# A hybrid diffusion layer on one core: the MLP's scale as a factor per partition, and two transposes moved into the output projection

## Chip, core and metric

The kernel runs on one core of a Trainium2 chip. The metric is the device time of one execution in microseconds (us). The engines are named as in the profile: PE (matrix products and transposes, with PEld for its weight loads), DVE (vector), ACT (scalar), POOL, and SP, which only issues DMAs here; ACT issues a few as well.

## What is computed

One layer over 512 latent tokens of width 1024 with 256 context tokens. Two sub-layers follow each other: attention beside a state-space scan with a common output projection, then a gated MLP with a width-3 convolution along the tokens on the gate.

```python
mix_x = jnp.concatenate([attn_x, ssd_x], axis=-1) @ w_out[l]           # (512, 2048) @ (2048, 1024)
x = x + mod_x[2] * rms_norm(mix_x, mix_post_norm[l])
ffn_x = conv_glu(modulate(rms_norm(x, ffn_pre_norm[l]), mod_x[3], mod_x[4]),
                 w_up[l], ffn_conv_w[l], ffn_conv_b[l], w_down[l])
x = x + mod_x[5] * rms_norm(ffn_x, ffn_post_norm[l])

def rms_norm(x, w):     # y = x * rsqrt(mean(x*x) + EPS) * w
def modulate(h, shift, scale):
    return h * (1 + scale) + shift
```

`mod_x[i]` are six vectors of 1024 that one matrix-vector product makes from the conditioning vector: 2 is the mixer's gate, 3 the MLP's shift, 4 the MLP's scale, 5 the MLP's gate. All is float32.

## The kernel before

**Precision.** A float32 operand of a large product is split into two parts, hi and lo, in a format that PE takes at full rate (`split`, L497 on ACT makes hi, L498 on DVE makes lo), and a product is the sum of hi·hi, hi·lo and lo·hi.

**Order.** The program is built twice. The first build records every instruction; `plan` then gives each tile a place in SBUF and each engine an order, by list scheduling with costs and waits written into the kernel; the second build follows that order. So an edit anywhere can move instructions everywhere. Two means bind the plan: `pins` say that certain products of PE come after others, and the PSUM bank that a `pget` hands out is decided by the order of the code (a queue of free banks: `pfree` puts a bank at its end).

**The output projection** (`natural_gemm`, L1288) multiplies 16 blocks of the concatenated 2048 features with w_out. Its result lies token by token: four token blocks `i` of 128, each in one of the four PSUM buffers of 128x1024 (kind "a"). The last four of the 16 are kept back and run block by block, so that block 0 is finished before block 3; block 3's tail runs in two halves of 512 columns. One half of a tail is 12 products of 128x512.

**The modulation vectors** are made meanwhile on DVE, 24 dot products of 128x1024 (L586, with loads of 512 KB each), as columns: feature p of block j is at partition p, column j of `mod`. `modfinish` (L1273) adds the bias and the norm's weights. Where a vector is needed along the free axis, it becomes a row: a DMA on ACT's queue writes the column to DRAM in pieces of four bytes (L1282, `mod_rows<-mod`), another reads it back to all partitions (L1284, `block<-mod_rows`, 512 KB). Before, this is done for the mixer's gate (`rows[2]`) and the MLP's scale (`rows[4]`); the MLP's shift stays a column.

**After each token block** `after_mix` (L1365) takes the sum of squares of the projection on ACT (L1347), 1/sqrt by a power on POOL (L521) with a Newton step on DVE (L522 to L528), multiplies by the gate's row (L1360; for block 3's second half L1362 and L1363), adds the residual stream (L1375), which is also written to DRAM (`held_rows`), takes its sum of squares, and multiplies by that factor and by the scale's row (L1379) to `hn`.

**Into the MLP.** `transposes` (L1384) turns `hn` of one token block to features on partitions: eight transposes on PE (L1387) to a PSUM buffer, then for each of the eight feature blocks hi with the shift as bias on ACT (L1390) and lo on DVE (L1391), into `h2`. All transposes come in the code after the output projection. The MLP's first product (`up`, L758) runs for three column blocks of w_up over tokens 0 to 255 first and then over 256 to 511, so it begins when blocks 0 and 1 are in `h2`.

## Time and profile before

| | |
|---|---|
| median of 3 runs | 986.82 us (985.85 to 990.34) |
| profiled execution, first to last instruction | 986.9 us; its own time is not given apart, and the span is within 0.1 us of the median |
| mean granted clock of PE | 0.992 |
| PE, PEld busy | 98%, 84% |
| DVE, ACT, POOL busy | 69%, 51%, 27% |
| output projection's last product, MLP's first | 607.8 us, 611.5 us |

Busy shares are means over stages of different kinds. In a row of a group stand line, engine, operation, tiles, shapes and count, then the busy time, the mean of one in ns, and the idle time just before with its cause. In a timeline row stand start and length, and in brackets how long the engine was idle before and what ended that. A "DMA to landing" is from the issue to the last byte. Matmuls are pipelined, and one's own length (390 ns) is more than the distance to the next.

### The profile page before, as it was taken

How to read it: one execution, taken by the hardware profiler on the slowest of the kernel's cores; microseconds unless marked ns; L12 is line 12 of the kernel's file. 1: busy time of each engine (PE TensorE's matmuls, PEld its weight loads, DVE VectorE, ACT ScalarE, POOL GpSimd, SP SyncE). 2: the span in 40 equal slices, each digit the busy share in tenths (PEclk: the TensorE clock that was granted, in tenths of full speed). 3: DMA queues.
4: the chain of work that ended last, by engine and by line, in shares of the span. 5: the costliest groups of instructions: out<-in, count | busy, mean ns of one | idle time of the engine just before them, and what ended most of it. 6: DMA issues, size and time to landing. Idle time of an engine off the chain costs nothing. (4 is left out here: it accounts for less than half of the span.)

```text
span 986.9 us, 14324 instructions
## 1 busy us (share of the span) xinstructions
PE 964.1 (98%) x5213; PEld 824.1 (84%) x5213; DVE 685.7 (69%) x1181; ACT 500.8 (51%) x996; POOL 265.0 (27%) x238
## 2 busy tenths in 40 slices
PE   8999999999999999999999998999999999999997
PEld 8888888888878878889888887988888888888885
DVE  5999877896889999878789948925244342583504
ACT  4555347548569786878786114823232242652001
POOL 0002103756599986566440001000000000000000
PEclk8999999999999999999999999999999999999999
DMA  9923211012331341334577576332222312444422
GB/s 345 376 96 114 75 43 59 23 43 62 84 98 55 105 113 36 100 96 108 149 274 272 175 155 247 129 107 86 107 86 93 120 54 75 128 144 140 144 86 106
DMA packets 47542, 121.07 MB, mean 123 GB/s; under 512 B 9057, under 2 KB 12017, under 8 KB 47473
## 3 DMA queue, kind: packets, MB, share of 16 engines
q1 hardware_dynamic: 43744, 118.49, 37.4%
q10 hardware_dynamic: 3728, 1.68, 0.6%
q8 instruction: 41, 0.67, 0.3%
q14 instruction: 29, 0.23, 0.1%
HBM read 98.11 MB, written 6.30 MB: 106 GB/s over the span
## 5 line engine op out<-in xcount | busy, mean ns | idle before, releaser
L758 PE MATMUL banks<-block,block 128*128 128x512 f32 (+1 forms) x2132 | 449.7, 362 | 4.3 <-ACT block L1390 1.9
L758 PEld LDWEIGHTS banks<-block,block 128*128 128x128 f32 x2132 | 361.8, 190 | 65.6 <-ACT block L1390 2.1
L498 DVE TENSOR_TENSOR block<-block,block 128x512 fp32r<-128x512 f32 (+5 forms) x252 | 217.8, 890 | 105.3 <-ACT block L497 44.6
L497 ACT ACTIVATE block<-block 128x512 fp32r<-128x512 f32 (+4 forms) x252 | 180.7, 746 | 204.8 <-PE banks L1482 43.0
L521 POOL TENSOR_TENSOR smalls<-smalls,powers 128x1 f32<-128x1 f32 (+3 forms) x16 | 12.7, 792 | 507.0 <-DVE smalls L1466 359.3
L1482 PE MATMUL banks<-block,block 128*128 128x512 f32 x512 | 117.8, 389 | 0.0
L1482 PEld LDWEIGHTS banks<-block,block 128*128 128x128 f32 x512 | 96.1, 188 | 19.9
L1188 POOL TENSOR_TENSOR block<-block,smalls 128x768 f32<-128x768 f32 x64 | 95.4, 1498 | 51.9 <-DVE smalls L1187 32.7
L1181 PE MATMUL banks<-block,block 128*128 128x256 f32 (+1 forms) x384 | 95.3, 355 | 5.1 <-issue 1.9
L498 DVE TENSOR_TENSOR block<-banks,block 128x512 fp32r<-128x512 f32 (+1 forms) x156 | 83.2, 556 | 13.9 <-ACT block L497 12.5
L1295 PE MATMUL banks<-block,block 128*128 128x512 f32 x384 | 89.2, 390 | 0.0
L497 ACT ACTIVATE block<-banks 128x256 fp32r<-128x256 f32 (+1 forms) x156 | 74.0, 500 | 23.3 <-PE banks L1199 10.8
L1295 PEld LDWEIGHTS banks<-block,block 128*128 128x128 f32 x384 | 71.6, 188 | 14.7 <-DVE block L1236 0.2
L1181 PEld LDWEIGHTS banks<-block,block 128*128 128x128 f32 x384 | 59.7, 189 | 13.0 <-ACT block L1185 4.4
L1211 PE MATMUL banks<-block,block 128*128 128x256 f32 x384 | 68.7, 294 | 0.1
L1185 ACT ACTIVATE block<-banks,smalls 128x768 f32<-128x768 f32 x64 | 58.0, 907 | 14.4 <-DVE smalls L1183 10.1
L1183 DVE TENSOR_REDUCE smalls<-banks 128x1 f32<-128x768 f32 x64 | 60.8, 950 | 5.9 <-PE banks L1181 5.6
L586 DVE SCALAR_TENSOR_TENSOR block<-block,block 128x1024 f32<-128x1024 f32 x50 | 60.3, 1219 | 6.2 <-DMA block<-in_wmod_dram 6.1
L1199 PE MATMUL banks<-cst,block 128*128 128x128 f32 x384 | 63.2, 273 | 0.1
L1211 PEld LDWEIGHTS banks<-block,block 128*128 128x128 f32 x384 | 56.4, 189 | 4.6 <-ACT block L497 1.1
L793 DVE SCALAR_TENSOR_TENSOR block<-banks,cwh,block 128x510 f32<-128x510 f32 (+3 forms) x88 | 51.7, 621 | 11.3 <-ACT block L789 10.5
L1199 PEld LDWEIGHTS banks<-cst,block 128*128 128x128 f32 x384 | 46.5, 140 | 8.1 <-issue 2.2
(220 smaller groups left out, 1040.8 us busy)
## 6 DMA issues: line engine op xcount, KB each, us to landing
block<-in_wmod_dram SPq DMA_DIRECT2D x48, 512.0 KB, 6.2
block<-in_wup_dram SPq DMA_DIRECT2D x44, 512.0 KB, 4.5
block<-in_wdn_dram SPq DMA_DIRECT2D x44, 256.0 KB, 3.3
block<-block SPq DMA_DIRECT2D x32, 256.0 KB, 3.0
block<-in_wout_dram SPq DMA_DIRECT2D x16, 512.0 KB, 5.2
block<-block SPq DMA_DIRECT2D x56, 128.0 KB, 2.5
block<-in_wxbc_dram SPq DMA_DIRECT2D x12, 512.0 KB, 3.3
block<-in_wz_dram SPq DMA_DIRECT2D x16, 256.0 KB, 6.0
```

Of the source, the lines that this page charges most:

```text
L497: act(hi, src, AF.Copy)
L498: (lo_eng or V).tensor_tensor(out=lo, in0=src, in1=hi, op=ALU.subtract)
L586: V.scalar_tensor_tensor(out=junk, in0=wt, scalar=0.5, in1=vec, op0=ALU.mult, op1=ALU.mult, accum_out=acc)
L758: mm(po, lhsT=wf(k, pt[0]), rhs=xf(k, pt[1]), start=(k == 0 and pt == parts[0]), stop=(k == nk - 1 and pt == parts[-1]))
L1181: mm(sc[:, o : o + n], lhsT=q_[:, x_, qi * P : (qi + 1) * P], rhs=kk[:, y_, :], start=part == 0, stop=part == 2)
L1183: V.reduce_max(nm, sc[:, :T], axis=AX.X, negate=True)
L1185: act(pe, sc[:, :T], AF.Exp, bias=nm, scale=1.0, accum_out=sm_)
L1188: G.tensor_tensor(out=pe, in0=pe, in1=sm_.to_broadcast([P, T]), op=ALU.mult)
L1199: nc.tensor.transpose((tx if c < NX else tc_)[:, o : o + P], pe[:, s_ : s_ + P], ident)
L1211: mm(po[:, half * 256 : half * 256 + 256], lhsT=vst(c), rhs=rhs, start=(part == 0 and c == 0), stop=(part == 1 and c == NKT - 1))
L1295: mm(po[i][:, nh * 512 : nh * 512 + 512], lhsT=l[lp][:, i * P : (i + 1) * P], rhs=w[wp][:, nh * 512 : nh * 512 + 512], start=(k == 0 and l ...
L1482: mm(po[i], lhsT=l[lp][:, i * P : (i + 1) * P], rhs=w[wp], start=(k == 0 and lp == 0 and wp == 0), stop=(k == NF - 1 and lp == 1))
```

## The change

There are four parts.

1. The MLP's scale (with ffn_pre_norm and 1 added) stays a column. `hn` is now only the normed stream, a multiplication by one factor per token (a TENSOR_SCALAR, L1383), and scale and shift are applied at the transposes' outputs, where features lie on partitions: one ACTIVATE with both columns to a new tile `ht` (L1394). The two DMAs for that row are gone.
2. hi and lo of `h2` are made from `ht` on DVE, for two feature blocks at a time, by a cast (L1398) and a subtraction (L1399). For that, `h2`'s tiles hold hi of two feature blocks or lo of two, in place of hi and lo of one.
3. `natural_gemm` calls `ahead` in front of each half of block 3's tail: the transposes of block 0 in front of the first half and those of block 1 in front of the second. Pins keep them there: the transposes come ahead of their half, and the second half behind the first. With that, block 0's and 1's transposes take the projection's buffers of blocks 0 and 1, and the MLP's first two column blocks get those of blocks 2 and 0, where they got those of blocks 2 and 3.
4. `rsqrt` puts half of its argument in a column of its own, so that DVE need not wait until POOL has read the argument.

```diff
     def rsqrt(x, n):
-        yt, tt = small(f"ry{n}", n), small(f"rt{n}", n)
+        yt, tt, xh = small(f"ry{n}", n), small(f"rt{n}", n), small(f"rh{n}", n)
         G.tensor_tensor(out=yt, in0=x, in1=powers[:, :n], op=ALU.pow)
-        V.tensor_scalar(out=x, in0=x, scalar1=-0.5, scalar2=None, op0=ALU.mult)
+        V.tensor_scalar(out=xh, in0=x, scalar1=-0.5, scalar2=None, op0=ALU.mult)
...
         for i in range(NX):
-            at.append(len(nc.cur_bb.bb.instructions))
-            cut = here()
-            for halves in (range(2),) if i < NX - 1 else ((0,), (1,)):
-                if halves == (1,):
-                    pins.append(((cut, here()), (here(), here() + 3 * len(tail))))
+            group, cut = [], here()
+            for n, halves in enumerate((range(2),) if i < NX - 1 else ((0,), (1,))):
+                between = here()
+                if i == NX - 1:
+                    ahead(n)
+                began = here()
                 for k, w, l in tail:
                     one(k, i, w, l, halves)
-            at[-1] = at[-1], len(nc.cur_bb.bb.instructions)
+                group.append((began, here()))
+                pins.extend(((o, o + 1), group[-1]) for o in range(between, began))
+            pins.extend(zip(group, group[1:]))
+            at.append((cut, here()))
             done(i, po[i])
...
         for h in cuts:
-            V.scalar_tensor_tensor(out=hn[:, h], in0=x1[i][:, h], scalar=c1, in1=rows[4][:, h], op0=ALU.mult, op1=ALU.mult)
+            V.tensor_scalar(out=hn[:, h], in0=x1[i][:, h], scalar1=c1, scalar2=None, op0=ALU.mult)
...
+        ht = t4(P, KD, P)
         for k in range(KD):
-            hi, lo, b = h2[k][:, 0, i * P : (i + 1) * P], h2[k][:, 1, i * P : (i + 1) * P], mod[:, 24 + k : 25 + k]
-            act(hi, tp[:, k * P : (k + 1) * P], AF.Identity, bias=b)
-            V.scalar_tensor_tensor(out=lo, in0=tp[:, k * P : (k + 1) * P], scalar=b, in1=hi, op0=ALU.add, op1=ALU.subtract)
+            act(ht[:, k], tp[:, k * P : (k + 1) * P], AF.Identity, scale=mod[:, 32 + k : 33 + k], bias=mod[:, 24 + k : 25 + k])
         pfree(tp)
+        for k in range(0, KD, 2):
+            hi, lo = (h2[k + p_][:, :, i * P : (i + 1) * P] for p_ in range(2))
+            V.tensor_copy(hi, ht[:, k : k + 2])
+            V.tensor_tensor(out=lo, in0=ht[:, k : k + 2], in1=hi, op=ALU.subtract)
...
-                rows[src] = modfinish(n, src, add, nrm, src != 3)
-
-    natural_gemm(16, lambda k: weight(a["wout"][korder[k]]), out_operand, after_mix, beside_out, keep=4)
+                rows[src] = modfinish(n, src, add, nrm, src == 2)
+
+    natural_gemm(16, lambda k: weight(a["wout"][korder[k]]), out_operand, after_mix, beside_out, keep=4,
+                 ahead=lambda n: transposes(*tails[n]))
...
-    h2v = lambda k, p_: h2[k][:, p_, :]
+    h2v = lambda k, p_: h2[k // 2 * 2 + p_][:, k % 2, :]
...
-    transposes(*tails[0])
-    transposes(*tails[1])
```

What the plan makes of it is shown at three places. PE before, at the end of the output projection (L1295), where block_916 is block 0's `hn`, block_920 block 1's, and L758 the MLP:

```order
L1295 MATMUL banks<-block_900_5539,block_879_5483 128x512
L1295 MATMUL banks<-block_901_5540,block_879_5483 128x512
L1295 MATMUL banks<-block_900_5539,block_888_5521 128x512
L1387 MATMUL banks<-cst,block_916_5584 128x128 x4
L1387 MATMUL banks<-cst,block_920_5621 128x128 x4
L1387 MATMUL banks<-cst,block_916_5584 128x128 x4
L1387 MATMUL banks<-cst,block_920_5621 128x128 x4
L758 MATMUL banks<-block_876_5478,block_935_5771 128x256
L758 MATMUL banks<-block_876_5478,block_941_5829 128x256
```

PE after, at the first transposes (L1391, block_915 is block 0's `hn`):

```order
L1295 MATMUL banks<-block_497_3054,block_696_4427 128x512
L1295 MATMUL banks<-block_875_5474,block_680_4345 128x512
L1295 MATMUL banks<-block_899_5535,block_902_5539 128x512 x2
L1295 MATMUL banks<-block_497_3054,block_697_4428 128x512
L1295 MATMUL banks<-block_876_5475,block_680_4345 128x512
L1391 MATMUL banks<-cst,block_915_5581 128x128 x4
L1295 MATMUL banks<-block_660_4179,block_697_4428 128x512
L1295 MATMUL banks<-block_875_5474,block_878_5478 128x512
L1391 MATMUL banks<-cst,block_915_5581 128x128 x4
L1295 MATMUL banks<-block_848_5367,block_654_4136 128x512
```

Block 0's transposes stood behind every product of the projection; now 38 products stand behind them. Block 1's stand 14 products ahead of the end. Behind the end (the first of the rows below is the last product), the MLP begins with four products, and then block 2's transposes follow (block_925 is its `hn`):

```order
L1295 MATMUL banks<-block_899_5535,block_902_5539 128x512
L758 MATMUL banks<-block_497_3054,block_942_5826 128x256
L758 MATMUL banks<-block_497_3054,block_936_5769 128x256
L758 MATMUL banks<-block_497_3054,block_939_5774 128x256
L758 MATMUL banks<-block_497_3054,block_945_5831 128x256
L1391 MATMUL banks<-cst,block_925_5666 128x128 x4
```

Before, block 2's first transposes stood behind 27 products of the MLP. Block 3's stand behind 59 products and block 2's eight transposes now.

ACT before, from the gate's scatter on (block_808 receives the gate's row, block_727 the scale's; L497 makes hi of w_out in block_900 and of w_up in block_935 and block_941; L1347 is a sum of squares):

```order
L1282 DMA mod_rows<-mod 128x8x1
L497 ACTIVATE block_900_5539<-block_779_5074 128x1024
L1347 ACTIVATE block_789_5114,smalls<-banks 128x1024
L1282 DMA mod_rows<-mod 128x8x1
L1284 DMA block_808_5191<-mod_rows 128x1024
L497 ACTIVATE block_935_5771<-block_809_5193 128x1024
L1284 DMA block_727_4691<-mod_rows 128x1024
L497 ACTIVATE block_941_5829<-block_744_4752 128x1024
```

ACT after (block_792 receives the gate's row; block_936 and block_942 are hi of w_up; L1351 is the sum of squares):

```order
L497 ACTIVATE block_897_5531<-block_715_4583 128x512
L1282 DMA mod_rows<-mod 128x8x1
L1351 ACTIVATE block_715_4583,smalls<-banks 128x1024
L497 ACTIVATE block_936_5769<-block_114_661 128x1024
L497 ACTIVATE block_942_5826<-block_799_5154 128x1024
L1284 DMA block_792_5143<-mod_rows 128x1024
L1351 ACTIVATE block_797_5150,smalls<-banks 128x1024
L497 ACTIVATE block_939_5774<-block_789_5113 128x1024
```

Of four DMAs two are left, and two conversions of w_up stand between the gate's scatter and its broadcast now.

DVE before, from the gate's row to block 0's `hn` (block_916; L1360 multiplies by the row, L1375 adds the residual stream, L1379 makes `hn`; the single-column rows are the Newton steps):

```order
L1360 TENSOR_TENSOR block_798_5151<-banks,block_808_5191 128x1024
L1375 SCALAR_TENSOR_TENSOR block_798_5151<-block_798_5151,smalls,block_715_4582 128x1024
L498 TENSOR_TENSOR block_936_5772<-block_809_5193,block_935_5771 128x1024
L1349 TENSOR_SCALAR smalls<-smalls 128x1
L522 TENSOR_SCALAR smalls<-smalls 128x1
L524 SCALAR_TENSOR_TENSOR smalls<-smalls 128x1
L528 SCALAR_TENSOR_TENSOR smalls<-smalls 128x1
L1349 TENSOR_SCALAR smalls<-smalls 128x1
L1360 TENSOR_TENSOR block_918_5612<-banks,block_808_5191 128x1024
L522 TENSOR_SCALAR smalls<-smalls 128x1
L1379 SCALAR_TENSOR_TENSOR block_916_5584<-block_798_5151,smalls,block_727_4691 128x1024
```

DVE after, the last part of the same stretch (ahead of it stand L1364 and L1379 of block 0, the first by the row, the second the residual stream's addition; L1383 makes `hn`):

```order
L1364 TENSOR_TENSOR block_843_5333<-banks,block_792_5143 128x1024
L524 SCALAR_TENSOR_TENSOR smalls<-smalls 128x1
L1353 TENSOR_SCALAR smalls<-smalls 128x1
L528 SCALAR_TENSOR_TENSOR smalls<-smalls 128x1
L522 TENSOR_SCALAR smalls<-smalls 128x1
L1379 SCALAR_TENSOR_TENSOR block_843_5333<-block_843_5333,smalls,block_597_3790 128x1024
L524 SCALAR_TENSOR_TENSOR smalls<-smalls 128x1
L498 TENSOR_TENSOR block_943_5827<-block_799_5154,block_942_5826 128x1024
L528 SCALAR_TENSOR_TENSOR smalls<-smalls 128x1
L1353 TENSOR_SCALAR smalls<-smalls 128x1
L1383 TENSOR_SCALAR block_915_5581<-block_818_5230,smalls 128x1024
```

Block 1's addition of the residual stream (L1379 after, L1375 before) now stands ahead of block 0's `hn`; there are six operations of 1024 columns from the row to `hn` where there were five.

More of the change, by code (lines that the diff above doesn't have):

```diff
@@ L518, in rsqrt @@
     def rsqrt(x, n):
-        yt, tt = small(f"ry{n}", n), small(f"rt{n}", n)
+        yt, tt, xh = small(f"ry{n}", n), small(f"rt{n}", n), small(f"rh{n}", n)
         G.tensor_tensor(out=yt, in0=x, in1=powers[:, :n], op=ALU.pow)
-        V.tensor_scalar(out=x, in0=x, scalar1=-0.5, scalar2=None, op0=ALU.mult)
+        V.tensor_scalar(out=xh, in0=x, scalar1=-0.5, scalar2=None, op0=ALU.mult)
         if n == 1:
-            V.scalar_tensor_tensor(out=tt, in0=yt, scalar=yt, in1=x, op0=ALU.mult, op1=ALU.mult)
+            V.scalar_tensor_tensor(out=tt, in0=yt, scalar=yt, in1=xh, op0=ALU.mult, op1=ALU.mult)
         else:
             V.tensor_tensor(out=tt, in0=yt, in1=yt, op=ALU.mult)
-            V.tensor_tensor(out=tt, in0=tt, in1=x, op=ALU.mult)
+            V.tensor_tensor(out=tt, in0=tt, in1=xh, op=ALU.mult)
         V.scalar_tensor_tensor(out=yt, in0=tt, scalar=1.5, in1=yt, op0=ALU.add, op1=ALU.mult)
@@ L1285, in modfinish, with natural_gemm @@
         return row
-    def natural_gemm(nk, wf, lf, done, beside_=lambda k: None, keep=4):
+    def natural_gemm(nk, wf, lf, done, beside_=lambda k: None, keep=4, ahead=lambda n: None):
         po = [pget("a") for _ in range(NX)]
@@ L1403, in beside_out @@
             if k == 4 * n + 3:
-                rows[src] = modfinish(n, src, add, nrm, src != 3)
-    natural_gemm(16, lambda k: weight(a["wout"][korder[k]]), out_operand, after_mix, beside_out, keep=4)
+                rows[src] = modfinish(n, src, add, nrm, src == 2)
+    natural_gemm(16, lambda k: weight(a["wout"][korder[k]]), out_operand, after_mix, beside_out, keep=4,
+                 ahead=lambda n: transposes(*tails[n]))
     gT = []
     EARLY = 3
-    h2v = lambda k, p_: h2[k][:, p_, :]
+    h2v = lambda k, p_: h2[k // 2 * 2 + p_][:, k % 2, :]
     def up(j, pu, ws, lo, hi):
         for s_ in range(2):
-            gemm_T(blk(ws[s_]), KD, ((pu[:, s_ * 512 + lo : s_ * 512 + hi], lambda k, p_: h2[k][:, p_, lo:hi]),))
+            gemm_T(blk(ws[s_]), KD, ((pu[:, s_ * 512 + lo : s_ * 512 + hi], lambda k, p_: h2v(k, p_)[:, lo:hi]),))
     def gated(j, gate, other, used):
```

## The prediction

> **What bounds the kernel now.** I read the page first, then busy time by stretch, then the PE timeline where a stretch falls short, then the chain that ended last to see what that place waits for.
>
> ```profile
> span 986.9 us, 14324 instructions
> PE 964.1 (98%) x5213; PEld 824.1 (84%) x5213; DVE 685.7 (69%) x1181; ACT 500.8 (51%) x996; POOL 265.0 (27%) x238
> L1295 PE MATMUL banks<-block,block 128*128 128x512 f32 x384 | 89.2, 390 | 0.0
> ```
>
> PE is busy for 964.1 of 986.9 us, so the end is set by PE's work and by the places where PE stands still or runs slowly. In the output projection it loses nothing: 384 products in 89.2 us, 0.232 us each. The stretches around the step from there to the MLP (columns: length, PE, PEld, DVE, ACT, POOL, then the granted clock):
>
> ```profile
> 600.00:605.00 5.00, 5.00 (x23) 4.13 (x23) 3.99 (x9) 2.15 (x4) 0.55 (x1) 1.00 0.75 238
> 605.00:610.00 5.00, 4.67 (x29) 3.87 (x27) 3.61 (x8) 2.40 (x4) 0.55 (x1) 1.00 0.58 230
> 610.00:615.00 5.00, 1.75 (x5) 1.26 (x6) 3.83 (x10) 2.93 (x10) 2.17 (x3) 0.76 0.95 336
> 615.00:620.00 5.00, 5.00 (x29) 5.00 (x27) 4.26 (x15) 4.56 (x15) 0.72 (x2) 0.55 0.36 143
> 620.00:625.00 5.00, 5.00 (x44) 4.94 (x42) 5.00 (x15) 4.52 (x12) 0.00 (x0) 1.00 0.08 9
> 625.00:630.00 5.00, 5.00 (x44) 5.00 (x43) 5.00 (x15) 4.69 (x12) 0.00 (x0) 1.00 0.93 369
> ```
>
> ```profile
> 599.81 8.10 PE L1295 MATMUL banks<-block,block 128*128 128x512 f32 x35
> 607.75 1.91 PE L1387 MATMUL banks<-cst,block 128*128 128x128 f32 x16
> 611.53 0.39 PE L758 MATMUL banks<-block,block 128*128 128x256 f32 x1 [1.87 <-ACT block L1390]
> 613.23 0.79 PE L758 MATMUL banks<-block,block 128*128 128x256 f32 x2 [1.31 <-DVE block L1360]
> 614.43 5.35 PE L758 MATMUL banks<-block,block 128*128 128x256 f32 x24 [0.40 <-DVE block L1391]
> ```
>
> Here lies what can be won. At 607.75 the last product is out, 16 transposes of blocks 0 and 1 follow, and then PE has nothing it may do: it waits 1.87 us for the first eviction, 1.31 us for a bank that block 3's reader still holds, 0.40 us for a low part. After these gaps the clock is 0.55 until 620, and matmuls come at 29 per 5 us instead of 44. From 610 to 625 there are 5 + 29 + 44 = 78; at 44 per 5 us they need 8.9 us, so 6.1 us are lost, with the 0.33 idle before 610 **6.5 us**. That is the ceiling of the main term. The chain says what comes before it:
>
> ```profile
> 563.79 10.08 DMA mod_rows<-mod
> 573.89 17.18 DMA block<-mod_rows
> ...
> 623.90 236.28 PE banks L758 x1154
> ```
>
> The mixing gate's row goes out as a column at 563.79 and comes back as a broadcast at 591.07. All of after_mix hangs on that arrival; from 623.9 on PE is the chain.
>
> **The second row.** The MLP's scale no longer becomes a row: one scatter, one broadcast and the two waits on ACT for them go.
>
> ```profile
> 571.54 1.30 SPq L489 DMA_DIRECT2D block<-in_wup_dram  x1
> ```
> ```profile
> 571.79 0.37 ACTq L1282 DMA_DIRECT2D mod_rows<-mod  x1
> ...
> 583.03 1.06 ACT L497 ACTIVATE block<-block 128x1024 fp32r<-128x1024 f32 x1 [10.69 <-DMA block<-in_wup_dram]
> 590.63 0.34 ACTq L1284 DMA_DIRECT2D block<-mod_rows  x1
> 591.09 1.06 ACT L497 ACTIVATE block<-block 128x1024 fp32r<-128x1024 f32 x1 [7.00 <-DMA mod_rows<-mod]
> ```
> ```profile
> DMA to landing us min/median/max: 6.0/11.0/18.8
> ```
>
> The last row is that of the tile mod_rows. The first broadcast's 17.2 us ended within half a microsecond of the second scatter, which stood ahead of it in ACT's queue (571.79 to 590.6). The broadcast that had nothing ahead took 6.0. So the remaining one should take about 6.0 to 6.5 instead of 17.2. But it starts later, for two reasons. In DVE's new order one L586, one L498 of 1024 and one of 512 more stand ahead of the gate's last factor (1.22 + 1.22 + 0.7 = 3.1 us): scatter at 567.0. And in ACT's new order two conversions of w_up stand between scatter and broadcast, where before there was none; ACT takes these in turn, so the broadcast waits for a load. Loads hardly move after a scatter; these two stretches of 4 us, from 572 and from 580, show it:
>
> ```profile
> DMA packets 19, 0.08 MB, mean 19 GB/s; under 512 B 0, under 2 KB 0, under 8 KB 19
> ...
> DMA packets 797, 1.46 MB, mean 365 GB/s; under 512 B 441, under 2 KB 441, under 8 KB 797
> ```
>
> Of before, the load issued at 571.54, the fourth in that jam, landed as its reader started, at 583.0: 19.2 after the scatter. After, the load that ACT needs is the third (or the second) of the jam; at 0.5 MB per 365 GB/s each place is 1.4 us. So it lands at 567.0 + 19.2 - 1.4 = 584.8 at the latest, and if loads move as soon as the scatter lands (10.08) at 567.0 + 10.1 + 3 x 1.4 = 581.3. Plus one conversion (1.06) and 6.0 to 6.5: the row arrives between **588.4 and 592.4**; I take 591.3, nearer the late end, since the jam is a row and its early end is not.
>
> **From the row to the first transposes.** DVE's rows for the steps between:
>
> ```profile
> L498 DVE TENSOR_TENSOR block<-block,block 128x1024 fp32r<-128x1024 f32 x77 | 93.5, 1225 | 43.7 <-PE banks L758 23.3 <-ACT block L497 18.0 <-issue 1.8
> L586 DVE SCALAR_TENSOR_TENSOR block<-block,block 128x1024 f32<-128x1024 f32 x50 | 60.3, 1219 | 6.2 <-DMA block<-in_wmod_dram 6.1
> L1083 DVE TENSOR_SCALAR block<-block,smalls 128x512 f32<-128x512 f32 x4 | 4.2, 1043 | 0.0
> L1375 DVE SCALAR_TENSOR_TENSOR block<-block,smalls,block 128x1024 f32<-128x1024 f32 x3 | 3.9, 1284 | 0.1
> L1379 DVE SCALAR_TENSOR_TENSOR block<-block,smalls,block 128x1024 f32<-128x1024 f32 x3 | 3.8, 1282 | 0.1
> L1360 DVE TENSOR_TENSOR block<-banks,block 128x1024 f32<-128x1024 f32 x3 | 3.7, 1217 | 8.2 <-DMA block<-mod_rows 8.2
> L667 DVE TENSOR_SCALAR cc<-c 128x512 f32<-128x512 f32 x1 | 0.4, 421 | 0.0
> ```
> ```profile
> 597.53 1.28 DVE L1379 SCALAR_TENSOR_TENSOR block<-block,smalls,block 128x1024 f32<-128x1024 f32 x1
> ```
>
> Before, block 0's hn was done at 598.81, 7.7 us after the row: five long operations (1.22 + 1.28 + 1.23 + 1.22 + 1.28 = 6.2) and 1.4 of small ones and waits. After, six stand there: L1364, L1379, L1364, L1379, L498 and the new TENSOR_SCALAR (5 x about 1.24 = 6.2, plus it). Its price is not in the trace at 1024 elements. At 512 it is 0.42 (L667) or 1.04 (L1083, while POOL was at work); 0.7 to 2.1 for 1024. I take 0.7, since POOL has only single columns to do here. So hn comes 6.2 + 0.7 + 1.4 = 8.3 after the row: at **599.6** (596.7 to 602.1).
>
> [...]
>
> PE must have that hn when it comes to the new place of the transposes, 38 products ahead of the projection's end: 607.75 - 38 x 0.232 = **598.9**. So PE waits 0.7 us there (0 to 3.2). Block 1's transposes stand 14 products before the end, at about 605, while its hn follows by one L498 and one factor: no wait.
>
> **The evictions.** ACT now does eight with scale and bias per block, DVE four casts and four subtractions of 256 in place of eight L1391. None of the three is in the trace.
>
> ```profile
> L789 ACT ACTIVATE block<-banks,cbh,cwh 128x512 f32<-128x512 f32 x12 | 9.4, 784 | 18.9 <-PE banks L758 18.7
> L1390 ACT ACTIVATE block<-banks,mod 128x128 fp32r<-128x128 f32 x32 | 9.7, 368 | 3.3 <-DVE block L1391 2.7 <-PE banks L1387 0.2
> L627 ACT ACTIVATE block<-banks 128x512 f32<-128x512 f32 x1 | 0.6, 597 | 4.5 <-PE banks L534 4.5
> ```
>
> Two columns add 784 - 597 = 187 ns, one about 94. An L1390 takes 9.7 / 32 = 0.30 in sequence, so the new one 0.30 to 0.40: 2.4 to 3.2 us per block. A cast and a subtraction of 256 are at most half of L667's and L498's times at 512 and 1024 plus their fixed part, some 0.3 + 0.4; four pairs 2.8, against 8 x 0.29 = 2.4 before. DVE has spare time for it (3.83 of 5 us at 610), and L1379's five instructions become cheaper ones. Block 0's evictions lie beside the 38 products and cost nothing; without that cover they cost the 1.87 us of now. Block 1's start after the square of block 3's first half on ACT, 12 products and four transposes (3.2 us) before PE comes to the MLP; the first pair is ready about 1 us ahead of it. What is late next: block 2's transposes stand four products into the MLP and need block 1's bank, which its eighth eviction frees between 0.0 and 0.8 us after PE gets to the MLP; PE is there at 0.5. And block 3's stand 59 products (6.7 us) and 8 transposes in, while its chain through ACT, POOL (L1367 behind seven L521) and DVE ends 7 to 8 us in. Together 0.4 us (0 to 1.0). No product waits for block 3's bank any more: the 1.31 us go.
>
> SP's held_rows writes and w_up loads keep their places among each other, and none of PE's three waits above was for a load; I count nothing for them. The separate half in rsqrt takes L522 (0.15 us) off the last chain: nothing that can be measured.
>
> **The sum.** 6.5 - 0.7 - 0.4 = 5.4 us. The profiled execution (986.9) is the median (986.82) to 0.1 us. Forecast: 986.8 - 5.4 = **981.4 us**.
>
> **Rivals.**
>
> A, *the row comes late* (slower). The broadcast is now queued on ACT behind a load. The place is the first transposes, with 38 products and the whole MLP behind them on PE. It decides from a wait of 6.1 us, a row at 596.7, or of 3.2 (593.8) if the clock falls too (B). For it: 17.18 for such a broadcast, with w_up loads beside it. At 584.8 + 1.1 + 17.2 = 603.1, hn is there at 611.4, PE waits 12.5 us and then runs a slow stretch (below, 2.9): 986.8 - 6.5 + 12.5 + 2.9 + 0.4 = **996.1**. Against it: what made it 17.2 is removed. 0.16.
>
> B, *the short wait costs the clock*. A wait of 1 to 2 us brings a slow stretch: 610 to 620 shows one whose loss beyond the idle 3.6 us is 6.5 - 3.6 = 2.9. Then 6.5 - 1.5 - 2.9 - 0.4 = 1.7: **985.1**. Against it stands the longest gap inside the attention:
>
> ```profile
> 490.85 0.47 PE L1181 MATMUL banks<-block,block 128*128 128x512 f32 x1 [1.91 <-issue]
> ```
> ```profile
> 490.00:493.00 3.00, 2.15 (x14) 1.93 (x15) 1.56 (x4) 1.55 (x5) 1.47 (x1) 1.00 1.02 348
> ```
>
> 1.91 us, and the clock stays 1.00; only the 3.6 us within 4.8 at 610 brought it down. [...]
>
> C, *another plan elsewhere*. The planner sets the whole program's order anew, so other stalls appear. From 300 to 500 PE is idle for
>
> ```profile
> 300.00:500.00 200.00, 194.53 (x1281) 171.08 (x1281) 173.34 (x320) 158.74 (x374) 137.69 (x114) 1.00 0.38 104
> ```
>
> 5.5 us, in gaps of which the longest is that 1.91. If a new plan has twice that, the gain is gone: 986.8 - 5.4 + 5.5 = **986.9**. Nothing speaks for more or for fewer. 0.14.
>
> **How the numbers follow.** The forecast's case has 0.58, of which 0.46 lie below 981.9, that is faster by over 0.5% (about what a measurement of this kernel can tell from no change), and 0.12 above. B (0.12) is within; C gives 0.10 within and 0.04 slower; A 0.06 within and 0.10 slower. Faster 0.46, same 0.40, slower 0.14. The range goes from the whole 6.5 us with 2 us of luck in the new plan (978.5) through B and C to A's milder half (989.0).
>
> **What would show it.** Right: PE's timeline has the first eight transposes at about 599 with a gap of under 2 us ahead, L758 starts within 1 us of the last product, the clock stays 1.00 through 610 to 620, and mod_rows shows two scatters and a broadcast of 6 to 7 us. Wrong: the row lands after 594, a slow stretch follows the wait, or PE's idle time grows in stretches that the change does not touch.

## The result, and the profile after

| | before | after |
|---|---|---|
| first measurement, median (range) | 986.87 us (985.85 to 990.34, 6 runs) | 978.6 us (6 runs, 978.06 to 980.02 and one of 1059.55), ratio 0.9918 [0.9902, 0.9934] |
| second measurement | 987.52 us (984.78 to 989.38, 13 runs) | 978.48 us (978.25 to 979.34, 4 runs), ratio 0.9917 [0.9896, 0.9937] |
| profiled execution, span | 986.9 us | 976.3 us |

After is 8.3 to 9.0 us faster. The profile of after shown here is that of the second measurement, since the execution of 1059.55 us, the profiled one of the first, ran at a mean granted clock of 0.847. The page of after:

```profile
span 976.3 us, 14332 instructions
PE 957.4 (98%) x5213; PEld 817.2 (84%) x5213; DVE 693.0 (71%) x1181; ACT 503.3 (52%) x996; POOL 272.8 (28%) x238
```

PE has the same 5213 instructions and is busy for 6.7 us less. Busy time by stretch at the step, after (columns as before; the last two are DMA's share and GB/s):

```profile
605.00:610.00 5.00, 5.00 (x41) 4.79 (x39) 4.14 (x11) 3.92 (x12) 1.82 (x2) 1.00 0.48 193
610.00:615.00 5.00, 5.00 (x45) 5.00 (x44) 4.45 (x15) 4.72 (x11) 0.66 (x1) 1.00 0.66 213
615.00:620.00 5.00, 5.00 (x44) 5.00 (x44) 4.97 (x11) 5.00 (x11) 0.00 (x0) 1.00 0.26 103
```

Where 1.75 of 5 us were busy and then the clock stood at 0.55, PE is now busy throughout at full clock, with 45 and 44 matmuls per 5 us. PE's timeline at the same place:

```profile
595.50 0.60 PE L1391 MATMUL banks<-cst,block 128*128 128x128 f32 x4
595.85 0.71 PE L1295 MATMUL banks<-block,block 128*128 128x512 f32 x2
596.40 0.60 PE L1391 MATMUL banks<-cst,block 128*128 128x128 f32 x4
...
606.00 0.63 PE L758 MATMUL banks<-block,block 128*128 128x256 f32 x4
606.47 0.60 PE L1391 MATMUL banks<-cst,block 128*128 128x128 f32 x4
```

No row here has a bracket: PE waits neither at block 0's transposes (595.50) nor at the MLP's first product (606.00) nor at block 2's transposes (606.47). What came before on DVE and ACT:

```profile
585.57 1.23 DVE L1364 TENSOR_TENSOR block<-banks,block 128x1024 f32<-128x1024 f32 x1 [6.90 <-DMA block<-mod_rows]
...
592.33 0.75 DVE L1383 TENSOR_SCALAR block<-block,smalls 128x1024 f32<-128x1024 f32 x1
```
```profile
577.93 1.06 ACT L497 ACTIVATE block<-block 128x1024 fp32r<-128x1024 f32 x1 [6.27 <-DVE block L586]
577.96 0.34 ACTq L1284 DMA_DIRECT2D block<-mod_rows  x1
...
596.93 2.90 ACT L1394 ACTIVATE block<-banks,mod 128x128 f32<-128x128 f32 x8 [0.46 <-PE banks L1391]
```

The row is there at 585.5, block 0's `hn` at 593.1, 2.4 us ahead of PE, and ACT waits for PE at the evictions and not PE for ACT.

To compare programs whose start differs, I use one measure below: from the start of PE's 3400th instruction (counted from 0), a product of the output projection ahead of all transposes of `hn` in every program here, to the start of its last. It holds the step and the MLP. Worked out from the traces:

| program | time, median (us) | 3400th at | from there to the last |
|---|---|---|---|
| before | 985.8 to 987.5 | 595.7 | 383.7 |
| before's order with part 4's column | 985.4 | 593.0 | 382.9 |
| before, second order | 983.7 | 595.6 | 379.0 |
| before, third order | 984.4 | 592.8 | 380.8 |
| part 4 alone | 995.0 | 597.2 | 390.0 |
| parts 1, 2, 4 | 985.1 | 590.8 | 385.4 |
| part 3 alone | 981.0 | 591.9 | 379.9 |
| after | 978.5 | 592.1 | 377.0 |
| after, `hn` of block 0 later | 981.5 | 592.8 | 379.2 |
| after, second order | 987.8 | 594.5 | 384.6 |
| after, one conversion ahead | 989.3 | 591.7 | 387.4 |
| after, third order | 981.0 | 595.1 | 377.1 |
| after, another price of a scatter | 977.8 | 591.9 | 376.9 |

377 us is what this part takes when PE loses nothing at the step. Of the 10.6 us between the two profiled spans, 6.7 lie here, and 3.6 had been won by the 3400th instruction, 2.2 of them by the 200th (36.8 us before, 34.6 after). One profiled execution stands behind each row, and they differ: in before's order the measure was 383.7 in one and 382.9 in another, that with part 4's column, so the gain at the step is 5.9 to 6.7.

### The profile page after: what moved, and what is told of

Read it like the earlier page. It is cut to its first block, busy times and chain, and to the rows that moved or that the text cites. A ratio compares the mean times of both kernels' runs of the same rounds, so it can differ in the third digit from the quotient of the medians.

```text
span 1057.5 us, 14332 instructions
## 1 busy us (share of the span) xinstructions
PE 1043.8 (99%) x5213; PEld 855.8 (81%) x5213; DVE 694.7 (66%) x1181; ACT 505.5 (48%) x996; POOL 267.7 (25%) x238
## 4 chain that ended last, share of the span: by engine, by line
PE 95%; DVE 2%; DMA 1%; issue 1%; ACT 0%; POOL 0%; DVEq 0%; SPq 0%; ACTq 0%
PE banks L758 43%; PE banks L1488 13%; PE banks L1295 9%; PE banks L1181 6%; PE banks L685 5%; PE banks L1211 5%; PE banks L1199 4%; PE banks L1115 2%; PE banks L1064 1%; PE banks L1016 1%; PE banks L1056 1%; PE banks L596 1%; DVE block L498 1%; PE banks L1031 1%; PE banks L808 1%; PE banks L1035 1%
## 5 line engine op out<-in xcount | busy, mean ns | idle before, releaser
L758 PE MATMUL banks<-block,block 128*128 128x512 f32 (+1 forms) x2132 | 485.8, 382 | 0.2
L758 PEld LDWEIGHTS banks<-block,block 128*128 128x128 f32 x2132 | 370.6, 194 | 83.8 <-DVE block L498 1.2
L498 DVE TENSOR_TENSOR block<-block,block 128x512 fp32r<-128x512 f32 (+5 forms) x252 | 229.3, 938 | 79.3 <-ACT block L497 32.3
L497 ACT ACTIVATE block<-block 128x512 fp32r<-128x512 f32 (+4 forms) x252 | 180.3, 743 | 175.4 <-DMA block<-in_wdn_dram 35.1
L521 POOL TENSOR_TENSOR smalls<-smalls,powers 128x1 f32<-128x1 f32 (+3 forms) x16 | 13.7, 853 | 549.3 <-DVE smalls L1472 392.4
L1488 PE MATMUL banks<-block,block 128*128 128x512 f32 x508 | 130.1, 417 | 0.0
L1488 PEld LDWEIGHTS banks<-block,block 128*128 128x128 f32 x508 | 97.6, 192 | 29.9
L1181 PE MATMUL banks<-block,block 128*128 128x512 f32 (+1 forms) x384 | 101.4, 372 | 0.0
L1295 PE MATMUL banks<-block,block 128*128 128x512 f32 x384 | 99.3, 419 | 0.0
L498 DVE TENSOR_TENSOR block<-banks,block 128x256 fp32r<-128x256 f32 (+1 forms) x156 | 82.6, 556 | 13.2 <-ACT block L497 11.2
L1295 PEld LDWEIGHTS banks<-block,block 128*128 128x128 f32 x384 | 73.2, 192 | 21.4
L497 ACT ACTIVATE block<-banks 128x256 fp32r<-128x256 f32 (+1 forms) x156 | 74.6, 498 | 32.3 <-PE banks L1199 16.3
L1199 PE MATMUL banks<-cst,block 128*128 128x128 f32 x384 | 71.5, 291 | 0.7 <-DVE block L498 0.6
L1211 PE MATMUL banks<-block,block 128*128 128x256 f32 x384 | 72.1, 307 | 0.1
L1181 PEld LDWEIGHTS banks<-block,block 128*128 128x128 f32 x384 | 63.7, 196 | 7.3 <-ACT block L1185 0.6
L1211 PEld LDWEIGHTS banks<-block,block 128*128 128x128 f32 x384 | 59.4, 195 | 5.8 <-issue 0.9
L1429 ACT ACTIVATE block<-banks,prm 128x512 f32<-128x512 f32 x22 | 16.6, 777 | 98.6 <-PE banks L758 98.6
L586 DVE SCALAR_TENSOR_TENSOR block<-block,block 128x1024 f32<-128x1024 f32 x50 | 60.1, 1221 | 1.5 <-DMA block<-in_wmod_dram 1.4
```

Source lines behind the costliest of these rows:

```text
L497: act(hi, src, AF.Copy)
L498: (lo_eng or V).tensor_tensor(out=lo, in0=src, in1=hi, op=ALU.subtract)
L586: V.scalar_tensor_tensor(out=junk, in0=wt, scalar=0.5, in1=vec, op0=ALU.mult, op1=ALU.mult, accum_out=acc)
L758: mm(po, lhsT=wf(k, pt[0]), rhs=xf(k, pt[1]), start=(k == 0 and pt == parts[0]), stop=(k == nk - 1 and pt == parts[-1]))
L1181: mm(sc[:, o : o + n], lhsT=q_[:, x_, qi * P : (qi + 1) * P], rhs=kk[:, y_, :], start=part == 0, stop=part == 2)
L1199: nc.tensor.transpose((tx if c < NX else tc_)[:, o : o + P], pe[:, s_ : s_ + P], ident)
```

## The experiments

In the expectations S says that the gain is made at the step, by the move and by what frees the first transposes, P that it lies in the rest of the new order, and Q, formed later, that what decides is which instruction stands on ACT ahead of those that PE needs. Where a kernel has added lines, the line numbers of its profile are a little higher than after's.

**The parts apart.** After again, and three kernels with some of the parts:

> The changed kernel again, for a profile at full clock: the profiled run of it had a granted clock of 0.847 throughout. Time 978.6 us, within 1. Theory S (the step into the MLP): PE's idle time and the slow clock between the projection's end and the MLP, 6.5 us before, are gone, so PE between about 598 and 625 us shows under 1 us of idle and the clock 1.00, and the other 1.8 us of the 8.3 lie elsewhere. Theory P (another plan): at least 4 of the 8.3 us are idle time that vanished in stretches that the change does not touch (before 500 us or after 860 us).

> The scale as a factor per partition, the casts and the rsqrt column, but blocks 0 and 1 are transposed behind the last product as before. S: the first eviction and block 3's bank are waited for again (1.9 and 1.3 us) and the clock falls again, so 984 to 987 us. P: the plan is new, so anything from 977 to 987, with PE's idle time at the step no guide to the total.

> The transposes of blocks 0 and 1 ahead of the two halves of block 3's tail, with the scale's row, its two DMAs and the old evictions kept. S: most of the gain, 980 to 983 us, with a wait of 0 to 3 us at the first transposes, because both rows are needed for them and the second broadcast lands at about 597. If the second row is what delays block 0, the wait at the first transposes is over 3 us and the clock falls: 984 to 987. P: no order among these kernels.

> Only the separate column for the halved argument in rsqrt; nothing else changes but that the plan is made anew. S: 986.9 us less at most 0.3, plus or minus what a new plan does, which I put at 1.5 us. P: the plan alone moves it by 3 us or more.

Parts 1, 2 and 4 without the move:

```diff
-    natural_gemm(16, ..., after_mix, beside_out, keep=4,
-                 ahead=lambda n: transposes(*tails[n]))
+    natural_gemm(16, ..., after_mix, beside_out, keep=4)
...
+    transposes(*tails[0])
+    transposes(*tails[1])
     begun = []
```

985.07 us, ratio 0.998 [0.9966, 0.9994]: nearly nothing, and at the step it is worse than before (385.4 against 383.7). PE, then ACT there:

```profile
602.80 1.91 PE L1391 MATMUL banks<-cst,block 128*128 128x128 f32 x16
609.28 1.11 PE L1391 MATMUL banks<-cst,block 128*128 128x128 f32 x4 [4.56 <-ACT block L1394]
```
```profile
607.80 0.63 ACT L1351 ACTIVATE block<-block 128x512 f32<-128x512 f32 x1 [2.04 <-DVE block L1379]
```

Amid the evictions that PE waits for, ACT stands at a sum of squares of block 3, which DVE has not yet prepared.

Part 3 alone is after's `natural_gemm` and its call, with before's row for the scale, evictions and `rsqrt`: 980.95 us, ratio 0.9936 [0.9914, 0.9959]. The second row's scatter and broadcast stay, and block 0's `hn` is ready at 594.3, 1.1 us ahead of PE, so no wait comes of it. The move alone brings most of the gain in the order it got.

Part 4 alone is the diff of `rsqrt`: 995.04 us, ratio 1.0083 [1.0062, 1.0105]. It was forecast at nothing. On ACT, then DVE:

```profile
594.15 1.06 ACT L497 ACTIVATE block<-block 128x1024 fp32r<-128x1024 f32 x1 [14.31 <-DMA block<-in_wup_dram]
594.34 0.33 ACTq L1284 DMA_DIRECT2D block<-mod_rows  x1
```
```profile
600.57 1.28 DVE L1379 SCALAR_TENSOR_TENSOR block<-block,smalls,block 128x1024 f32<-128x1024 f32 x1 [2.96 <-DMA block<-mod_rows]
```

The scale's broadcast stood on ACT behind a conversion that waited 14.31 us for its load of w_up, and block 0's `hn` came 3 us late for it. That is rival A's mechanism, on the other row. But PE did not wait for this `hn`. PE, then ACT at the step:

```profile
609.22 1.91 PE L1387 MATMUL banks<-cst,block 128*128 128x128 f32 x16
617.62 1.23 PE L758 MATMUL banks<-block,block 128*128 128x256 f32 x4 [6.49 <-ACT block L1390]
```
```profile
612.37 1.06 ACT L497 ACTIVATE block<-block 128x1024 fp32r<-128x1024 f32 x1 [5.18 <-DMA block<-in_wup_dram]
...
616.46 0.36 ACT L1390 ACTIVATE block<-banks,mod 128x128 fp32r<-128x128 f32 x1
```

The transposes followed the last product without a gap, and PE then waited 6.49 us for the evictions. These began 7.2 us after the transposes, where before it was 3.1: on ACT a conversion that waited 5.18 us for its load, three sums of squares and a second conversion stood ahead of them. The late row had its part in this only through DVE, which had the first of these sums ready at 611.9. How the loss divides between the two is not shown.

**Is it the column or the order?** Before's plan is kept, and only the second build has the column:

```diff
-        yt, tt = small(f"ry{n}", n), small(f"rt{n}", n)
+        yt, tt, xh = small(f"ry{n}", n), small(f"rt{n}", n), small(f"rh{n}", n)
+        if places is None:
+            xh = x
```

> Before with part 4 alone again (the half of rsqrt's argument in a column of its own), but with the order and the places in SBUF that the planner found for before: the planner doesn't see the new column. Part 4 with an order of its own took 995.0 us against 987.5. S (the 7.5 us came from the new order: its second row's broadcast stood on ACT behind a conversion of w_up, was issued at 594.3 and DVE waited for it until 600.6): 987.5, within 1.5 us. R (the column itself costs, since POOL and DVE now work side by side): 993 or more.

985.4 us (983.42 to 988.64, 10 runs), ratio 0.9984 [0.997, 0.9998]. The column costs nothing and gains a little (0.2 to 3.0 us by the interval). The column can't account for the 7.5 us of part 4 alone; they came with the new order that the planner made for it. So every edit here carries the price of a new order, and the next runs measure that.

**The same programs in other orders.** One number of the planner's cost model is changed; the computation is not:

```diff
-    return (130 if len(ops) == 4 else 69) + 1.04 * n
+    return (130 if len(ops) == 4 else 69) + 1.045 * n
```

> Before, with one number of the planner changed: it takes 1.045 ns per element of DVE's operations for 1.04. Nothing that is computed changes, only the order. S (each new order moves the whole by several us): not 987.5, but anywhere from 983 to 995; here block 0's and 1's transposes still stand behind the whole projection, and 3 to 7 us are idle or slow there. P (the order has little weight): 987.5, within 1 us.

> After, with the same number of the planner changed (1.045 for 1.04). The gate's broadcast now stands on ACT behind a sum of squares alone, with no conversion of w_up between. S (moving the transposes takes away the stall of the step under any order in which the row comes by about 594): no gap over 1 us and no half clock at the step, 977 to 983, and 6 to 7 us less than the other one has lost there. P (after's order is a lucky one): 984 or more, with a stall at the step.

With 1.035 for 1.045:

> Before, with 1.035 ns per element in the planner for DVE's operations (1.04 in before, 1.045 in the second order). Before has taken 986.4 to 987.5 in its first order and 983.7 in its second. S: 984 to 990, with 3 to 7 us idle or slow at the step, since the planner puts all sixteen transposes behind the projection's last product here. P (any order, any time): 980 to 995.

> After, with 1.035 ns per element in the planner. After has taken 978.5 in its first order and 987.8 in its second. On ACT the sixteen evictions of blocks 0 and 1 now stand behind three conversions of w_up and four sums of squares that come after the gate's row. Q (the evictions' place on ACT decides): a gap ahead of the MLP's first product if one of the three conversions gets its load after 597, none if they get it before; 978 to 982 without a gap, 985 to 989 with one. S (moving the transposes is enough): 977 to 982.

| planner's ns per element | before | after |
|---|---|---|
| 1.04 | 985.8 to 987.5 | 978.5 |
| 1.045 | 983.71 (981.18 to 986.06), 0.9971 [0.9955, 0.9988] | 987.82 (986.47 to 989.3), 1.0018 [1.0005, 1.003] |
| 1.035 | 984.37 (982.5 to 987.32), 0.9986 [0.9971, 1.0002] | 980.98 (980.04 to 981.8), 0.9943 [0.9928, 0.9957] |

The ratios are to before in its own order. S fell: the change wins 8 to 9 and 3.4 us in two orders and loses 4.1 in one. Nor does the step cost 3 to 7 us in each of before's orders, as S had it: in the second the measure is 2.0 above 377, in the third 3.8. After in its second order, PE at the MLP's first product and ACT ahead of it:

```profile
613.59 1.23 PE L758 MATMUL banks<-block,block 128*128 128x256 f32 x4 [4.87 <-DVE block L1398]
```
```profile
598.38 1.06 ACT L497 ACTIVATE block<-block 128x1024 fp32r<-128x1024 f32 x1 [0.96 <-DMA block<-in_wup_dram]
602.49 1.06 ACT L497 ACTIVATE block<-block 128x1024 fp32r<-128x1024 f32 x1 [3.04 <-DMA block<-in_wup_dram]
...
604.45 2.90 ACT L1394 ACTIVATE block<-banks,mod 128x128 f32<-128x128 f32 x8
```

The row came early enough and block 0's transposes ran at 598.01 without a wait. But two conversions of w_up stood on ACT ahead of block 0's evictions and waited for loads, so the evictions began 6.4 us after the transposes. PE then waited 4.87 us and ran at half clock for 6.8 us. In the third order one such conversion stands there too:

```profile
597.36 1.06 ACT L497 ACTIVATE block<-block 128x1024 fp32r<-128x1024 f32 x1 [3.41 <-DMA block<-in_wup_dram]
...
600.01 2.90 ACT L1394 ACTIVATE block<-banks,mod 128x128 f32<-128x128 f32 x8 [0.59 <-ACT block L1351]
```

Its load came after the 597 from which Q expected a gap, and still nothing was lost (377.1): that bound was taken from after's first order, and PE reached the transposes 3 us later here, at 598.54. So Q missed by its own bound, and as S expected the same time, this run does not tell the two apart. Before, in its second order, shows the other side on PE:

```profile
606.66 1.04 PE L1387 MATMUL banks<-cst,block 128*128 128x128 f32 x8
607.45 1.19 PE L1295 MATMUL banks<-block,block 128*128 128x512 f32 x4
608.48 1.04 PE L1387 MATMUL banks<-cst,block 128*128 128x128 f32 x8
609.27 5.06 PE L758 MATMUL banks<-block,block 128*128 128x256 f32 x40
```

There four products and eight transposes are all that covers the first evictions, and PE goes on into the MLP without a gap. A far smaller cover than 38 products was enough in this order, where ACT began the evictions at 607.57, 0.91 us after the first transposes.

**The mechanism by itself.** After's order is kept, and on ACT one conversion of w_up is moved from behind the evictions of blocks 0 and 1 to ahead of them:

```diff
+        moved = next(n for n in act_order[act_order.index(last_):] if n in halved)
+        act_order.remove(moved)
+        act_order.insert(act_order.index(first), moved)
         for order in planned[2].values():
```

> After, with one instruction moved: ACT's next conversion of w_up (L497) stands ahead of the eight evictions of block 0's transposes and not behind block 1's. All other places in the order are kept. That conversion writes a tile that the projection's last dozen products still read, so it can't run before about 605, and the evictions behind it start at about 606 and not at 596.9. Q (the step costs nothing only while nothing late stands ahead of the evictions on ACT, as in after under the other order, where conversions waited there for loads of w_up): PE waits about 5.4 us ahead of the MLP's first product and the clock halves for 6.8 us (2.9 us lost), 978.5 + 8.3 = 986.8. P (what counts lies elsewhere in the order): 978.5 to 980.

989.3 us (987.92 to 990.07, 10 runs), 1.003 [1.0021, 1.004] of before: one moved instruction costs 10.8 us. ACT, then PE:

```profile
605.09 1.06 ACT L502 ACTIVATE block<-block 128x1024 fp32r<-128x1024 f32 x1 [9.04 <-PE banks L1300]
606.05 2.89 ACT L1400 ACTIVATE block<-banks,mod 128x128 f32<-128x128 f32 x8
```
```profile
613.80 1.22 PE L763 MATMUL banks<-block,block 128*128 128x256 f32 x4 [8.07 <-DVE block L1404]
```

Q holds in kind, and was 2.5 us too low in size: the evictions began at 606.05 as expected, but the casts of block 1 also stand on DVE behind block 2's `hn`, so PE waited 8.07 us and not 5.4, and the half clock lasted 10.2 us and not 6.8. What the conversion itself waited for was no load this time but PE, 9.04 us, so here being late was enough, whatever the reason.

**How much later may `hn` be?** After's order is kept, with six more multiplications on DVE:

```diff
+        if i == 0 and places is not None:
+            for _ in range(6):
+                V.tensor_scalar(out=hn, in0=hn, scalar1=1.0, scalar2=None, op0=ALU.mult)
```

> After, with the planned order kept, and block 0's hn multiplied by 1 six times more on DVE (0.67 us each in sequence), so that it is ready 4.0 us later. It was done at 593.1 and PE came to its transposes at 595.5, so there are 2.4 us to spare: PE should wait 1.6 us at the first transposes. S with the clock unharmed: 978.5 + 1.6 = 980.1. S with rival B's mechanism (a wait of 1 to 2 us halves the clock for at least one stretch of 3.4 us): 981.8 with one stretch, 983.5 with two. P (the gain is not made at this step): 978.5, since a wait there would not matter.

981.48 us (980.18 to 982.28, 4 runs). DVE, then PE:

```profile
592.52 4.34 DVE L1390 TENSOR_SCALAR block<-block 128x1024 f32<-128x1024 f32 x6
```
```profile
596.91 0.66 PE L1398 MATMUL banks<-cst,block 128*128 128x128 f32 x4 [0.51 <-DVE smalls L525]
...
608.63 0.73 PE L761 MATMUL banks<-block,block 128*128 128x256 f32 x4 [1.01 <-DVE block L1405]
```

In this execution `hn` had 3.9 us to spare, so 4.3 us more cost 0.51 at the transposes, and 1.01 at the MLP, where DVE's casts were late too. The granted clock was 1.00 here from 600 to 630 us, so the time, which is near the 981.8 that was expected with one slow stretch, does not speak for rival B. The measure from the 3400th instruction grew by 2.2 us, of which the two waits are 1.5; the remaining 0.7 is not explained. The rest of the 3.0 us lies ahead of that instruction.

**A planner that knows of the jam.** The planner takes 5.0 us for a scatter; the gate's landed after 10.1 to 13.3 us in before, after and after's second order.

```diff
-DMA_START, DMA_WAIT, DMA_AHEAD, DMA_ALONE, DMA_WORDS = 650, 910, 3000, 0.8, 5000
+DMA_START, DMA_WAIT, DMA_AHEAD, DMA_ALONE, DMA_WORDS = 650, 910, 3000, 0.8, 11000
```

> After, with another number of the planner changed: it takes 11.0 us for a scatter of a column and not 5.0 (scatters landed 10.1 to 13.3 us after their issue, and loads stood still meanwhile). Without a stall at the step, after has needed 377.0 to 377.1 us from PE's 3400th instruction to its last in both orders that have none, and that instruction has come at 592 to 595. Q (a conversion that gets its load late, ahead of the evictions on ACT, makes the stall; a planner that knows of the late loads puts none there): no gap over 1 us at the step, 978 to 982. P (the price of the scatter has no part in it; each order is a draw): a stall is as likely as in the three orders so far, one of three; 985 to 989 with one.

977.81 us (977.17 to 978.29, 4 runs), ratio 0.9917 [0.99, 0.9933]; 376.9 from the 3400th instruction, no gap. It still puts a conversion ahead of the evictions, but one that waits for nothing:

```profile
596.09 1.05 ACT L497 ACTIVATE block<-block 128x1024 fp32r<-128x1024 f32 x1
597.04 2.89 ACT L1394 ACTIVATE block<-banks,mod 128x128 f32<-128x128 f32 x8
```

That fits Q, and it is the fastest version here, though not told apart from after. As one order it can't show that such a price makes every order good: two of the three others had no stall either.

## Why the prediction was right, step by step

The time (978.6) came out 0.1 us inside the fast edge of the range (978.5 to 989.0), on the side that had the highest chance; the forecast of 981.4 was 2.8 us too slow. The place and the mechanism of the gain were right. One part was luck: the prediction let block 0's evictions cost nothing because of the 38 products beside them, without reading what stood ahead of them on ACT. In this order nothing late did, but in after's second order it did.

**The ceiling, 6.5 us, was right.** From the 3400th instruction on, after is 6.7 us shorter than before (5.9 against the other execution of before's order). The 1.31 us for block 3's bank, the low part's 0.40, the first eviction's 1.87 and the slow stretch all went.

**The wait of 0.7 at the first transposes did not come.** PE was 3.6 us earlier at the 3400th instruction, so I add 3.6 to after's times to set them beside the forecast. The scatter (563.3 + 3.6 = 566.9 against 567.0) and PE's arrival at the transposes (595.5 + 3.6 = 599.1 against 598.9) were as forecast. After's DMAs by line from 545 to 600 (size, then median time to landing):

```profile
block<-mod_rows ACTq DMA_DIRECT2D x1, 512.0 KB, 7.5
mod_rows<-mod ACTq DMA_DIRECT2D x1, 4.0 KB, 13.3
```

The broadcast took 7.5, a little over the 6.0 to 6.5 allowed. It was issued at 577.96 + 3.6 = 581.6, where I had 582.4 to 585.9: the load of the conversion ahead of it landed at 577.85, 14.5 us after the scatter (14.3 to 17.8 forecast); its row names DVE's L586 instead, which itself had waited for a load and ended at the same time. The broadcast went out as that conversion began (577.96 against 577.93) and not as it ended (578.99). So the row was there at 585.5 + 3.6 = 589.1, inside the bounds of 588.4 to 592.4 but 2.2 ahead of the value taken. To choose the late end was the step that made the 0.7.

**From the row to `hn`** it took 7.6 us against 8.3. The new TENSOR_SCALAR of 1024 took 0.75, so the near row (L667, 0.42 at 512) was the right one and L1083 the wrong one. The evictions, by group:

```profile
L1394 ACT ACTIVATE block<-banks,mod 128x128 f32<-128x128 f32 x32 | 12.0, 479 | 0.5 <-PE banks L1391 0.5
L1399 DVE TENSOR_TENSOR block<-block,block 128x256 fp32r<-128x256 f32 x16 | 6.7, 421 | 0.3
L1398 DVE CAST block<-block 128x256 fp32r<-128x256 f32 x16 | 4.4, 288 | 0.0
```

12.0 / 32 = 0.375 each in sequence (0.30 to 0.40 forecast), and 0.29 + 0.42 for a pair on DVE (0.3 + 0.4 forecast).

**The 0.4 us behind the MLP's start** did not come either; PE has no gap over 0.3 us between 595 and 630. With the 0.7 these make 1.1 of the 2.8 us.

**The other 1.5 us lie outside the step** (0.2 are in the ceiling), and there two of the prediction's readings were off. It took the profiled execution of before for the median to 0.1 us. But timed runs are about 2 us above their own span (978.36 us at a span of 976.3 in after; 988.21 at 986.4 in one run of before), so the profiled 986.9 was, by this, one of before's longer executions, some 2 us above a middle one. That moves no term of the sum, but of the 3.6 us ahead of the 3400th instruction some 2 are this execution's. What made the 1.5 us is not shown. And rival C was priced by PE's small gaps alone. Over all the programs here the 3400th instruction came between 590.8 and 597.2, and the rest took between 376.9 and 390.0: the order weighs in both, and most at the step, which C had left out. Of after's four orders one, the second with 987.8, came out as C has it; four are too few to judge its chance of 0.14.

**Rival A was right in kind and wrong in place.** It had ACT's queue as the danger, with a load ahead of the broadcast. The runs had late instructions in other places as well: ahead of the evictions in after's second order (PE waited 4.87 us) and where the conversion was moved by hand (8.07). In part 4 alone they stood ahead of the broadcast and of the evictions, and PE waited 6.49 us for the evictions. The stall of before I read only from PE's side, as a wait for the first eviction. ACT in before:

```profile
606.97 1.06 ACT L497 ACTIVATE block<-block 128x1024 fp32r<-128x1024 f32 x1 [3.27 <-DMA block<-in_wup_dram]
608.66 1.06 ACT L1347 ACTIVATE block<-block 128x1024 f32<-128x1024 f32 x1 [0.63 <-DVE block L1375]
...
610.86 0.62 ACT L1390 ACTIVATE block<-banks,mod 128x128 fp32r<-128x128 f32 x2
```

The transposes began at 607.75, and the eviction came at 610.86 behind three sums of squares. The first of these waited until 608.66 for DVE's addition of the residual stream. The conversion ahead of it got its load late, but it had ended at 608.03, when only the first three of the 16 transposes had started, and ACT then stood idle until that sum. So it was not a load that held the eviction, but work of other blocks that stood ahead of it in the queue. The prediction's "without that cover they cost the 1.87 us of now" therefore priced only the moved transposes: with a late conversion on ACT, and the 38 products still there, the step cost 7.6 us (after's second order) and 10.4 us (the conversion moved) more than 377.

**What stays open.** The result holds for these two kernels in the orders they have. How much the change brings apart from its order is not settled: three orders of each give -8 to -9, +4.1 and -3.4 us. Whether part 3 needs parts 1 and 2 can't be told from one order of each either.

## What to carry to other kernels

When a planner sets the order, compare a change with the same program under a few harmless changes of the planner's numbers, before the gain or loss is put down to the change: here those alone moved one program by 9 us. When PE waits for an eviction, read what stood on the evicting engine ahead of it: here an instruction there that was not ready, because it waited for a load (3.04 us in after's second order) or for another engine (9.04 us with the conversion moved), held up the evictions behind it, and PE waited 4.87 and 8.07 us. Where a transfer lands late, its late time in the planner's costs is worth a try; the one order made with it here had no stall.

## What the runs showed of the hardware

**Half clock came behind a gap of 1.65 us, and not behind gaps of 1.91 and 2.59 us.** After has this gap at 279 us, and the clock in the stretch behind it (columns of the second: length, PE, granted clock, DMA share, GB/s):

```profile
280.67 1.52 PE L1016 MATMUL banks<-block,block 128*128 128x512 f32 x3 [1.65 <-DVE block L1021]
```
```profile
281.00:284.00 3.00, 3.00 (x8) 0.50 0.74 180
```

Behind a gap of 1.65 us, with one of 0.34 just ahead, came 3.4 us at half clock; from 100 to 300 us the mean is 0.99 there, and the same with `hn` later. Behind the 1.91 us at 488.9 in before the clock was 1.00 (490 to 493 us). At the start, after's third order has a gap of 2.59 us, and its clock is 1.00 from 8 to 20 us:

```profile
12.21 0.96 PE L616 MATMUL banks<-ones,block 128*128 128x64 f32 x7 [2.59 <-DVE block L610]
```

So half clock behind a short wait, which rival B expected at the step and which did not come there in after, is found in after at 281 us. The stretches at half clock last 3.4 us here, 6.8 at the step of before and in after's second order, 10.2 with the conversion moved and 13.7 in part 4 alone.

What the gaps differ in is not shown. At the step of before the clock fell at 612.64, within the gap of 1.31 us, so the prediction's three gaps are one too many: that of 0.40 us came after the fall.

**The same order does not start at the same clock.** From 12 to 16 us, before and then the run of before's order with part 4's column (columns as above):

```profile
12.00:16.00 4.00, 3.90 (x18) 0.50 1.03 407
```
```profile
12.00:16.00 4.00, 4.00 (x23) 0.57 1.04 404
```

The half clock lasted 6.8 us in the one and 3.4 in the other, and PE's 200th instruction (counted from 0) started at 36.8 and 34.8. Of after's order one profiled execution had none, one 3.4 us, and a third (with the conversion moved) none. That is about 2 us between executions of one order, of the 5.5 that before's timed runs spread over in one measurement (983.86 to 989.39).
